# A mixture-of-experts kernel: experts' outputs added to their tokens' rows in DRAM by an indirect transfer in place of one-hot products on TensorE

## The chip, the core and the metric

The kernel runs on one core of a Trainium2 chip. The metric is the device time of one execution in microseconds; the kernel before takes 2354.62 us, the median of three runs (2351.31 to 2360.58). The engines of the core are TensorE (PE; its weight loads are PEld), VectorE (DVE), ScalarE (ACT), GpSimd (POOL) and SyncE (SP). Each has its own queue of instructions and works through it in order; sixteen DMA engines move data for all of them.

## What is computed

The reference is two blocks of a language model, one after the other, for one sequence of 512 tokens (528 with 16 meta tokens) of width 1024, all in float32. The change concerns the end of the first block, a feed-forward layer in which each of 16 experts chooses its 66 tokens:

```python
def one_group(hs):
    logits = jnp.einsum('ld,de->le', hs, w_router, preferred_element_type=jnp.float32)
    aff = jax.nn.softmax(logits, axis=-1)
    g, idx = lax.top_k(aff.T, cap)                       # 16 experts, cap = 66 tokens each
    xg = hs[idx]
    a = jnp.einsum('ecd,edf->ecf', xg, w_gate)           # [1024, 2048] per expert
    u = jnp.einsum('ecd,edf->ecf', xg, w_up)
    y = jnp.einsum('ecf,efd->ecd', jax.nn.silu(a) * u, w_down)
    y = y * g[..., None].astype(y.dtype)
    out = jnp.zeros((L, D), y.dtype).at[idx.reshape(-1)].add(y.reshape(-1, D))
    return out.astype(hs.dtype)
...
h = h + expert_choice_ffn(rms_norm(h, ffn_norm_g[l]), w_router[l], w_gate[l], w_up[l], w_down[l])
```

Before it stand an attention and a convolution, whose projection gives `h`; behind it two more layers (an mLSTM layer and a latent attention) that read `h` in full.

## The kernel before, in words

**Precision.** Every weight and activation is split into two float32r parts, high and low, that sum to the float32 value; a product of two such pairs is three matmuls (`TRIPLES`, line 26). ACT writes the high part `wh` of a weight (line 164), DVE the low part `wl` as a difference (line 165).

**The weight stream.** All weights are one long list of items of 1 MB. `w_dma` (lines 117 to 140) issues an item's transfer on SP's queue into a slot; `w_cv` splits it into two halves of 128x1024, each of which takes one of four buffers of `wh` and of `wl`; `w_get` hands an item to the products, keeps one item split ahead and, among the experts, up to `K.ring` = 17 items in transfer or waiting. A slot comes free once DVE has read it. The last 48 items (two experts) have ten slots, because seven (`ex1`) are given to the next layer.

**The router** (`route`, lines 562 to 807) finishes `h` for each of four tiles of 128 tokens (`K.xs`, kept in SBUF) and for the 16 meta tokens, writes the normalised rows to DRAM as `hn_d` on ACT's queue (line 656), chooses the tokens, and leaves their positions `K.idx`, shifted positions `K.fi` and weights `K.gate`, one column for each expert.

**The experts** (`experts`, lines 905 to 1058). The order of TensorE's instructions is pinned to that of the program (`K.pin`); those of the other engines are put in order by the framework's scheduler. For each expert `e` and each half `f` of the hidden width, 48 products give G and 48 give U (66 rows by 1024 columns in PSUM); ACT takes silu of G into the tile `sa` (line 993), DVE multiplies it by U (line 999), and TensorE transposes the result (`rows_66`) for the 96 products of Y. In the middle of Y the tokens of the next expert, gathered by GpSimd into `xg` (`gather`, line 897, an indirect transfer by the list `K.idx`), are transposed.

**The sums** (lines 939 to 960). After Y, ACT and DVE split the 66 rows of Y, times their weight, into `yh` (in the buffer `xg`) and `yl` (in the buffer `sa`, of which there is one), and DVE builds a one-hot matrix `oh` from `K.fi`. For each of four tiles of tokens, four products of `oh` with `yh` and `yl` put the rows where their tokens stand, and DVE adds them to `K.xs`. The generator `left` is advanced inside the next expert's first half: three of the four tiles behind G's items 1 to 3, the fourth behind U's first item. After the fourth, `gather(K, e + 2)` is issued. The last expert's sums come in front of the second block, with a share of its work (lines 1024 to 1048).

Of the kernel before, what the change touches and what calls it, by code (L numbers as in the profile page):

```python
# [8 lines left out]
F32 = mybir.dt.float32  # L9
# [3 lines left out]
AF = mybir.ActivationFunctionType  # L13
OP = mybir.AluOpType
# [39 lines left out]
class Kern:  # L54
# [17 lines left out]
    def load_vecs(self, pool):  # L72
        """vectors whose elements go to partitions: rows of one tile, transposed"""
        nc, A = self.nc, self.A
        srcs = {"cw": A["conv_w"][0] if "conv_w" in A else None, "sg": A.get("attn_subln_g"),
                "acw": A["a_conv_w_2"][0], "acb": A["a_conv_b_2"], "ahg": A["a_h_norm_2"],
                "kvn": A["kv_norm_2"][None, :], "bn": A["b_norm_2"],
                "fg": A["ffn_norm_g"] if "ffn_norm_g" in A else None,
                "kg": A["k_gain_2"][None, 0:128], "qg": A["b_q_gain_2"][:, 0:128]}
        rows = self.t(pool, [128, 128], F32, "vrows")  # L80
        nc.gpsimd.memset(rows, 0.0)
        self.vcol = {}
        r = 0
        for n, src in srcs.items():
            if src is None:
                continue
            k = src.shape[0] * src.shape[1] // 128
            nc.gpsimd.dma_start(rows[r:r + k], src.rearrange("a (c p) -> (a c) p", p=128))
            self.vcol[n] = (r, k)
            r += k  # L90
        self.vrows = rows

    def vecs(self, ps):
        """called once the identity is there"""
        pt = self.t(ps, [128, 512], F32, "T", 2)
        self.nc.tensor.transpose(pt[:, :128], self.vrows, self.ident)
        self.vec = self.t(self.cst, [128, 128], F32, "vec")
        self.nc.vector.tensor_copy(self.vec, pt[:, :128])
# [14 lines left out]
    # ---- weights: raw float32 in, split into two float32r parts that sum to it exactly  # L113
# [98 lines left out]
    def rsqrt(self, pool, v, name):  # L212
        """1 / sqrt(v), by Newton steps"""
        nc = self.nc
        p, k = v.shape
        y = self.t(pool, [128, k], F32, name, 2)[:p]
        t = self.t(pool, [128, k], F32, name + "t", 2)[:p]
        nc.vector.tensor_single_scalar(y.bitcast(I32), v.bitcast(I32), 1, op=OP.logical_shift_right)
        nc.vector.tensor_scalar(y.bitcast(I32), y.bitcast(I32), -1.0, float(0x5f3759df), op0=OP.mult, op1=OP.add)
        nc.vector.tensor_scalar_mul(v, v, -0.5)  # L220
        for _ in range(3):
            nc.vector.tensor_mul(t, y, y)
            nc.vector.tensor_mul(t, t, v)
            nc.vector.scalar_tensor_tensor(y, t, 1.5, y, op0=OP.add, op1=OP.mult)
        return y

    def rstd(self, pool, ms, n, name):
        """ms [p, k] sums of squares over n -> 1/sqrt(ms/n + eps)"""
        p, k = ms.shape
        v = self.t(pool, [128, k], F32, name + "v", 2)[:p]  # L230
        self.nc.vector.tensor_scalar(v, ms, 1.0 / n, EPS, op0=OP.mult, op1=OP.add)
        return self.rsqrt(pool, v, name)


    def rsqrt_s(self, pool, v, name):
        """1 / sqrt(v) from ScalarE's square root and one Newton step"""
        nc = self.nc
        p, k = v.shape
        y, t = (self.t(pool, [128, k], F32, name + x, 2)[:p] for x in "yt")
        nc.scalar.activation(t, v, AF.Sqrt)  # L240
        nc.vector.reciprocal(y, t)
        nc.vector.tensor_mul(t, y, y)
        nc.vector.scalar_tensor_tensor(t, t, -0.5, v, op0=OP.mult, op1=OP.mult)
        nc.vector.scalar_tensor_tensor(y, t, 1.5, y, op0=OP.add, op1=OP.mult)
        return y

    def rstd_a(self, pool, ms, n, name):
        """the same from exp(-ln / 2) and one Newton step, where ScalarE has the tables of both"""
# [12 lines left out]
class Halves:  # L261
    """two tiles [128, n, ..], indexed as one [128, 2 n, ..]"""
# [23 lines left out]
def interleave(*gens):  # L286
    """gens: (generator, total cost); advances the one that is least far along"""
# [14 lines left out]
def block1(K):  # L302
# [26 lines left out]
    # ---- norm and transpose, a tile of tokens at a time, each followed by its values  # L329
# [18 lines left out]
    def values(pair, w, t):  # L348
# [3 lines left out]
        if m < 128:  # L352
            # both parts of the few tokens at once
# [42 lines left out]
    def proj_T(w, j, put):  # L396
        """channels 128 j .. of the chunk: put(columns, [128, 264] in PSUM) for each half of the tokens"""
# [138 lines left out]
    # lambda  # L536
# [25 lines left out]
def route(K, mixed, pa):  # L562
    """mixer output, router, expert choice, keys and values of the memory; starts the experts' weights"""
# [13 lines left out]
    K.hn_d = nc.dram_tensor("hn_d", [L, D], F32, kind="Internal").ap()  # L577

# [15 lines left out]
    # position of a token in two parts, its affinity in three, all of them exact in bfloat16  # L594
# [8 lines left out]
    # both parts of the few tokens side by side  # L603
# [10 lines left out]
    def mix(w, n, tiles):  # L614
        """columns 256 n .. of the mixer's output, for some tiles of tokens, the last head last"""
# [22 lines left out]
    def router(t):  # L638
        """affinities from h times the gain; 1 / rms comes in with the softmax"""
# [16 lines left out]
        nc.scalar.dma_start(K.hn_d[c0:c0 + m], hn[:m])  # L656
        lo = K.t(ps, [128, 512], F32, "Rl")
# [63 lines left out]
    # the CAP largest of each row, equal ones in order of position  # L721
# [33 lines left out]
    # every expert's slots against every expert's columns, then each expert's own  # L755
# [54 lines left out]
def mem_load(K, gain, mt):  # L810
    """the memory and its gain"""
# [5 lines left out]
def mem_norm(K, p, gain, mt, ms, junk=None):  # L817
    """a tile of the memory, normalised"""
# [7 lines left out]
def mem_keys(K, p, l, mks):  # L826
    """the keys of the memory, normalised, times their gain and the queries'"""
# [31 lines left out]
def expert_items(K):  # L859
    """weights of the memory's keys and values, of the experts"""  # L860
# [19 lines left out]
    # some slots have another use at the end  # L880
# [16 lines left out]
def gather(K, e, xg=None):  # L897
    """the tokens of expert e"""
# [6 lines left out]
def experts(K):  # L905
# [9 lines left out]
    def rows_66(src, dst):  # L915
        """[CAP, 1024] transposed and split: [128, 8 CAP]"""
# [22 lines left out]
    def sums(y, e, tags, after):  # L939
        """expert e's part of the sum, by a product with its one-hot rows: a generator of four steps"""  # L940
# [12 lines left out]
        for t in range(4):  # L953
# [4 lines left out]
            if t == 3:  # L958
                gather(K, e + 2)
            yield  # L960

    def mem_T(t):
        """a tile of the memory, transposed and split"""
# [12 lines left out]
    for e in range(K.ne):  # L976
# [5 lines left out]
        for f in range(2):  # L982
            g = K.t(ps, [128, 2, 512], F32, "G")
            for j in range(4):
# [5 lines left out]
                if f == 0 and j > 0:  # L990
                    next(left, None)
# [3 lines left out]
            for j in range(4):  # L995
                gemm(u, xx, 2 * j, get(), j == 0, j == 3)
                if f == 0 and j == 0:
                    next(left, None)
# [20 lines left out]
        left = sums(y, e, "GU" if last and K.fuse else "T", ins)  # L1019
        next(left)  # L1020
# [3 lines left out]
    if K.fuse:  # L1024
        # the second layer's keys and values of the memory, while the sums come together
# [35 lines left out]
def rows_T(K, ps, dst, src, cols):  # L1061
    """token-major src [128, 1024] -> dst (two parts) [:, 0:8, cols]"""
# [8 lines left out]
def mem_q(K, p, ps, w, hT, dst):  # L1071
    """a chunk of mq -> normalised, times 128 ** -0.5, transposed and split, for two heads; dst(j): where to"""
# [32 lines left out]
def mem_fetch(K, p, l, h, bufs=1, raw=("m_raw", 1)):  # L1105
    """keys and values of the memory for head h of layer l"""
# [9 lines left out]
def mem_attn(K, p, ps, kv, qT, dst, tp="m_pT"):  # L1116
    """a head of the memory attention, times dst / 2, into dst [128, 512]"""
# [28 lines left out]
def silu2(K, p, dst, src):  # L1146
    """2 silu(src) = (tanh(src / 2) + 1) src"""
# [5 lines left out]
def softmax_T(K, p, ps, s, scale, nb):  # L1153
    """rows of softmax(scale * s), [128, 128 nb] in PSUM, transposed: [128 keys, nb, 128] in PSUM"""
# [18 lines left out]
def acc4(K, ps, n):  # L1173
    """accumulators for the four tiles of tokens"""
# [4 lines left out]
def mm_part(K, acc, hT, k0, w, nk, first, last):  # L1179
    """acc[t] += hT[:, k0 ..]^T w"""  # L1180
# [9 lines left out]
# the chunks that come last have the last turn  # L1190
# [3 lines left out]
def out_proj(K, ps, mixed, his, rest, final):  # L1194
    """mixed^T @ w, in parts of 256 columns: final(t, n, psum); rest(c), a tile for the rest of chunk c"""
# [51 lines left out]
def a_pre(K):  # L1247
    """what the first layer can have before its input is there"""
# [10 lines left out]
    # gate weights: i in columns 0..3, f in 32..35  # L1259
# [27 lines left out]
def a_squares(K, t):  # L1287
    """h times its gain, and the sums of the squares before and after"""
# [9 lines left out]
def block2_a(K):  # L1298
# [31 lines left out]
    # x = rms_norm(h, final_norm_g); rmsnorm(x, a_norm); the values of the first head  # L1330
# [11 lines left out]
    for t in range(4):  # L1342
# [4 lines left out]
        # 1 / rms(h) and 1 / (rms(h) rms(x)) from the two sums  # L1347
# [28 lines left out]
    # gates, rows of heads  # L1376
# [17 lines left out]
    # log weight of s in t: (i_s - b_s) + R_S[t], R_S[t] = b_t - m_t + the sums of the tiles S .. T - 1  # L1394
# [176 lines left out]
    def rest(c):  # L1571
        # in place of the chunk before
# [15 lines left out]
def block2_b(K, out):  # L1588
# [11 lines left out]
    # the last two heads of both kinds take the place of values  # L1600
# [65 lines left out]
    # gains: rows of the rope part, columns of the rest  # L1666
# [28 lines left out]
    # rope tables  # L1695
# [28 lines left out]
    def rope_rows(pool, dst, src, heads):  # L1724
        """[128, 4, heads, 64]"""
# [11 lines left out]
    # latents of keys and values, of queries; the rope part that the keys share  # L1737
# [48 lines left out]
    def gen_q(pr):  # L1786
        """queries of two heads"""
# [22 lines left out]
    def gen_kv(pr):  # L1810
        """keys and values of two heads"""
# [43 lines left out]
    def gen_attn(pr):  # L1855
        qT, kT, qpT, kpT, v, rq = qkv[pr]
        for hh in range(2):
            # keys c of queries t in part t + 3 c
# [46 lines left out]
    def rest(c):  # L1905
        # in place of the chunk before
# [12 lines left out]
    def part(t, cs, one=False):  # L1919
        nonlocal prev  # L1920
        for c in cs:
            for i, (a, b) in enumerate(TRIPLES):
                beg, end = c == 0 and i == 0, c == ORDER[-1] and i == 2
                # of two tiles in a bank the first one opens it, the second one closes it
# [12 lines left out]
    def gen_out():  # L1937
        """the first part of the columns, as far as the chunks are there"""
# [106 lines left out]
```

## Time and profile before

| what | value |
|---|---|
| median of three runs | 2354.62 us (2351.31 to 2360.58) |
| span of the profiled execution | 2354.2 us (the runs' median is 0.42 us above it) |
| TensorE busy | 2277.8 us, 97% |
| TensorE's weight loads busy | 1707.0 us, 73% |
| DVE busy | 1838.8 us, 78% |
| ACT busy | 1456.0 us, 62% |
| GpSimd busy | 212.3 us, 9% |
| DMA | 520.27 MB, mean 221 GB/s |
| TensorE's granted clock | 0.985 in the mean |

A line of the timeline gives start, duration, engine, line of the kernel, operation, output<-input by the program's names, shape, and in brackets how long the engine had stood idle and what released it. The windows view gives for each stretch the busy time (and the number of instructions) of PE, PEld, DVE, ACT and POOL, the granted clock, the DMA engines' share and the rate. Matmuls are pipelined: the duration of one is longer than its share of a sequence, so the cost of a product is read from a group's length divided by its count.

### The profile page before, as it was taken

The page shows a single profiled execution, that of the slowest core. Times are in us where ns is not written, and L with a number is a line of the kernel's source. Part 1 is how long each engine was busy: PE and PEld are TensorE (multiplying, and loading weights), DVE is VectorE, ACT ScalarE, POOL GpSimd, SP SyncE. Part 2 cuts the span into 40 slices and gives each one's busy share as a digit, 9 for nine tenths or more (in the row PEclk, how much of TensorE's full clock was granted, in tenths as well). Part 3 has the DMA queues.
Part 4 walks back from the last instruction along what each step waited for, and adds up shares of the span by engine and source line. Part 5 has one row for each costly group of instructions (what it writes and reads, how often), then busy time and mean ns, then how long its engine had stood idle before and what let it go on. Part 6 is the DMA issues. An engine that isn't in the chain of part 4 may idle for free.

```text
span 2354.2 us, 33846 instructions
## 1 busy us (share of the span) xinstructions
PE 2277.8 (97%) x12647; PEld 1707.0 (73%) x12647; DVE 1838.8 (78%) x2704; ACT 1456.0 (62%) x2182; POOL 212.3 (9%) x227
## 2 busy tenths in 40 slices
PE   7999888999999999999999999999999999899999
PEld 7899884666666666666666666688888899777779
DVE  5766576999999999999999999876666756676752
ACT  4554345777777777777787777755453634555551
POOL 2201261000000000000000110241000000010000
PEclk9999997999999999999999999999999999999999
DMA  5211767999999999999999799542322233211122
GB/s 179 80 54 55 254 217 287 362 361 354 349 355 357 358 360 355 349 353 356 361 358 357 284 333 351 197 144 86 117 72 72 81 125 114 69 51 60 50 90 72
DMA packets 201553, 520.27 MB, mean 221 GB/s; under 512 B 12527, under 2 KB 94061, under 8 KB 201389
## 3 DMA queue, kind: packets, MB, share of 16 engines
q1 hardware_dynamic: 196157, 507.64, 60.3%
q0 software_dynamic: 3232, 7.77, 1.1%
q10 hardware_dynamic: 2000, 2.71, 0.3%
q8 instruction: 99, 1.62, 0.3%
q14 instruction: 65, 0.53, 0.1%
HBM read 504.31 MB, written 11.60 MB: 219 GB/s over the span
## 4 chain that ended last, share of the span: by engine, by line
PE 80%; DVE 2%; ACT 1%; issue 0%; DMA 0%; SPq 0%; ACTq 0%; DVEq 0%
PE P L198 23%; PE G L198 15%; PE U L198 15%; PE Y L198 15%; PE S L198 4%; PE O L198 3%; PE T L198 3%; PE T L203 1%; PE T L1169 0%; PE T L1843 0%; DVE wl L165 0%; PE T L1136 0%; DVE x L1293 0%; PE T L1067 0%; DMA xg<-hn_d,idx 0%
## 5 line engine op out<-in xcount | busy, mean ns | idle before, releaser
L164 ACT ACTIVATE wh<-raw 128x1024 fp32r<-128x1024 f32 (+1 forms) x604 | 632.6, 1054 | 292.0 <-PE P L198 69.1
L165 DVE TENSOR_TENSOR wl<-raw,wh 128x1024 fp32r<-128x1024 f32 (+1 forms) x586 | 705.5, 1223 | 121.8 <-ACT wh L164 115.9
L198 PE MATMUL G<-wh,xgT 128*66 128x512 f32 x1024 | 281.0, 396 | 0.7 <-ACT xgT L191 0.7
L198 PE MATMUL Y<-wh,hT 128*66 128x512 f32 x1024 | 278.4, 394 | 0.0
L198 PE MATMUL U<-wh,xgT 128*66 128x512 f32 x1024 | 278.2, 393 | 0.0
L164 ACT ACTIVATE wh<-h 128x1024 fp32r<-128x1024 f32 x200 | 210.3, 1059 | 63.2 <-PE G L198 22.5
L198 PE MATMUL P<-hT,wh 128*128 128x512 f32 x768 | 247.8, 396 | 0.0
L165 DVE TENSOR_TENSOR wl<-h,wh 128x1024 fp32r<-128x1024 f32 x196 | 234.2, 1220 | 13.0 <-ACT wh L164 11.2
L198 PEld LDWEIGHTS U<-wh,xgT 128*66 128x66 f32 x1024 | 140.2, 137 | 95.3
L198 PEld LDWEIGHTS G<-wh,xgT 128*66 128x66 f32 x1024 | 140.0, 138 | 94.6 <-issue 1.6
L198 PEld LDWEIGHTS Y<-wh,hT 128*66 128x66 f32 x1024 | 137.6, 137 | 90.2
L198 PEld LDWEIGHTS P<-hT,wh 128*128 128x128 f32 x768 | 143.6, 188 | 29.2
L198 PE MATMUL Y<-wl,hT 128*66 128x512 f32 x512 | 159.9, 394 | 2.2 <-DVE wl L165 2.2
L198 PE MATMUL G<-wl,xgT 128*66 128x512 f32 x512 | 160.9, 396 | 0.6 <-DVE wl L165 0.6
L198 PE MATMUL U<-wl,xgT 128*66 128x512 f32 x512 | 160.0, 394 | 0.0
L198 PE MATMUL P<-wh,hT 128*128 128x256 f32 (+2 forms) x712 | 147.2, 289 | 5.4 <-ACT hT L191 3.2
L198 PE MATMUL P<-hT,wl 128*128 128x512 f32 x384 | 151.4, 394 | 0.0
L198 PE MATMUL P<-h,wh 128*128 128x264 f32 x640 | 126.1, 290 | 1.6 <-ACT qraw L415 1.0
L165 DVE TENSOR_TENSOR wl<-mx,wh 128x1024 fp32r<-128x1024 f32 x96 | 118.0, 1247 | 8.6 <-ACT wh L164 7.5
L198 PEld LDWEIGHTS P<-wh,hT 128*128 128x128 f32 x712 | 116.2, 190 | 7.4 <-ACT hT L191 3.9
L164 ACT ACTIVATE wh<-mx 128x1024 fp32r<-128x1024 f32 x96 | 100.8, 1059 | 30.0 <-PE U L198 9.3
L198 PE MATMUL P<-wl,hT 128*128 128x256 f32 (+2 forms) x408 | 116.1, 287 | 0.0
(646 smaller groups left out, 4116.4 us busy)
## 6 DMA issues: line engine op xcount, KB each, us to landing
raw<-w_gate SPq DMA_DIRECT2D x82, 1024.0 KB, 6.9
raw<-w_down SPq DMA_DIRECT2D x80, 1024.0 KB, 7.1
raw<-w_up SPq DMA_DIRECT2D x76, 1024.0 KB, 6.9
h<-w_up SPq DMA_DIRECT2D x35, 1024.0 KB, 6.8
h<-w_down SPq DMA_DIRECT2D x32, 1024.0 KB, 7.3
h<-w_gate SPq DMA_DIRECT2D x31, 1024.0 KB, 6.9
raw<-a_w_in SPq DMA_DIRECT2D x24, 1024.0 KB, 5.3
mx<-w_up SPq DMA_DIRECT2D x17, 1024.0 KB, 7.2
```

The lines of the kernel that those rows point to most:

```text
L164: self.nc.scalar.activation(hv, v[:, r], AF.Copy)
L165: lo.tensor_tensor(lv, v[:, r], hv.bitcast(F32), op=OP.subtract)
L198: self.last_mm = self.nc.tensor.matmul(out, l, r, start=st, stop=sp)
L203: i = self.nc.tensor.transpose(out, src, ident)
```

## The change

Experts 0 to 14 no longer use products for their sums. The router also writes `h` to a DRAM tensor `acc_d`. After Y of an expert, ACT writes the rows times their weights to `ys` (in the buffer `sa`), and GpSimd issues one indirect transfer that adds the 66 rows of `ys` to the rows `K.idx` of `acc_d`; the gather for expert e + 2 is issued behind it. After the scatter of expert 14, four transfers on GpSimd's queue load the tokens' rows of `acc_d` back into `K.xs`. Expert 15 keeps the products. The rest of the diff takes comments and docstrings away.

```diff
@@ route @@
     K.hn_d = nc.dram_tensor("hn_d", [L, D], F32, kind="Internal").ap()
+    K.acc_d = nc.dram_tensor("acc_d", [L, D], F32, kind="Internal").ap()
...
         nc.scalar.dma_start(K.hn_d[c0:c0 + m], hn[:m])
+        nc.scalar.dma_start(K.acc_d[c0:c0 + m], h[t])
@@ experts @@
             nc.vector.tensor_add(K.xs[t], K.xs[t], o.rearrange("p a b -> p (a b)"))
-            if t == 3:
-                gather(K, e + 2)
             yield
 
+    def scatter(y, e):
+
+        ys = K.t(p, [CAP, 2, 512], F32, "sa")
+        nc.scalar.activation(ys, y[:CAP], AF.Copy, scale=K.gate[:, e:e + 1])
+        nc.gpsimd.indirect_dma_start(out=K.acc_d, out_offset=bass.IndirectOffsetOnAxis(ap=K.idx[:, e:e + 1], axis=0),
+                                     in_=ys.rearrange("p a b -> p (a b)"), in_offset=None, compute_op=OP.add)
+        gather(K, e + 2)
+        if e == K.ne - 2:
+            for t in range(4):
+                nc.gpsimd.dma_start(K.xs[t], K.acc_d[NM + 128 * t:NM + 128 * t + 128])
...
                 if f == 1 and j == 0:
                     rows_66(hh, hT[0])
-                if f == 0 and j > 0:
-                    next(left, None)
...
                 gemm(u, xx, 2 * j, get(), j == 0, j == 3)
-                if f == 0 and j == 0:
-                    next(left, None)
...
-        left = sums(y, e, "GU" if last and K.fuse else "T", ins)
-        next(left)
+        if last:
+            left = sums(y, e, "GU" if K.fuse else "T", ins)
+            next(left)
+        else:
+            scatter(y, e)
```

## Rows read from the trace of the kernel before

**Rows 1.** Windows of the experts' stage (columns as told above).
```profile
400.00:450.00 50.00, 50.00 (x230) 30.23 (x229) 47.10 (x44) 39.35 (x41) 0.00 (x0) 1.00 1.00 379
450.00:1300.00 850.00, 850.00 (x3893) 520.62 (x3892) 800.77 (x711) 651.77 (x652) 20.55 (x12) 1.00 0.97 355
```

**Rows 2.** The chain of waits, pieces in order of time: start, us, what.
```profile
479.47 11.08 PE U L198 x48
...
1411.58 11.09 PE U L198 x48
```

**Rows 3.** Timeline, SP's issues and ACT's first reads of the same slots.
```profile
510.02 3.14 SPq L138 DMA_DIRECT2D mx<-w_down  x2
...
557.65 1.06 ACT L164 ACTIVATE wh<-mx 128x1024 fp32r<-128x1024 f32 x1 [0.32 <-PE U L198]
...
1406.46 3.25 SPq L138 DMA_DIRECT2D mx<-w_down  x2
...
1431.49 3.89 ACT L164 ACTIVATE wh<-mx 128x1024 fp32r<-128x1024 f32 x4
```

**Rows 4.** DMA issues: queue, operation, count, KB each, median us to landing.
```profile
raw<-w_gate SPq DMA_DIRECT2D x82, 1024.0 KB, 6.9
...
mv_d<-mv POOLq DMA_DIRECT2D x1, 512.0 KB, 8.2
```

**Rows 5.** The tile xg: the sums' products, and the gather's landing times (ns min/median/max).
```profile
L198 PE MATMUL T<-xg,hT x120: 391/395/403, 447.3 to 1463.2; 66*128 66x512 f32 x120
...
L198 PE MATMUL T<-sa,hT x120: 388/395/427, 447.5 to 1463.4; 66*128 66x512 f32 x120
...
DMA to landing us min/median/max: 4.4/8.2/9.6
```

**Rows 6.** Timeline of PE: the end of Y, the first and the last group of sums.
```profile
513.03 0.62 PE L198 MATMUL Y<-wl,hT 128*66 128x512 f32 x2
...
519.01 0.40 PE L198 MATMUL T<-xg,hT 66*128 66x512 f32 x1
...
519.97 1.11 PE L198 MATMUL G<-wh,xgT 128*66 128x512 f32 x4
...
530.22 0.39 PE L198 MATMUL T<-xg,hT 66*128 66x512 f32 x1
...
531.14 1.07 PE L198 MATMUL U<-wh,xgT 128*66 128x512 f32 x4
```

**Rows 7.** Windows view of one period of an expert.
```profile
479.47:551.18 71.71, 71.71 (x329) 43.91 (x328) 67.58 (x61) 54.98 (x56) 1.71 (x1) 1.00 0.96 358
```

**Rows 8.** DVE's groups in that period that belong to the sums (busy us, mean ns).
```profile
L957 DVE TENSOR_TENSOR x<-x,T 128x1024 f32<-128x1024 f32 x4 | 4.9, 1213 | 0.0
...
L950 DVE SCALAR_TENSOR_TENSOR sa<-Y,gate,xg 66x512 fp32r<-66x512 f32 x2 | 1.5, 742 | 0.0
...
L945 DVE TENSOR_TENSOR hT<-iota,fi 66x512 fp32r<-66x512 f32 x1 | 0.7, 681 | 0.0
```

**Rows 9.** Timeline of ACT after the end of Y.
```profile
514.20 0.67 ACT L949 ACTIVATE xg<-Y,gate 66x512 fp32r<-66x512 f32 x1
```

**Rows 10.** Timeline around a silu in a half without sums.
```profile
478.84 0.62 PE L198 MATMUL G<-wl,xgT 128*66 128x512 f32 x2
...
480.01 1.00 ACT L993 ACTIVATE sa<-G 66x1024 f32<-66x1024 f32 x1
...
480.91 2.00 ACT L164 ACTIVATE wh<-raw 128x1024 fp32r<-128x1024 f32 x2
...
481.99 3.51 DVE L165 TENSOR_TENSOR wl<-raw,wh 128x1024 fp32r<-128x1024 f32 x3 [0.62 <-ACT wh L164]
...
485.74 0.64 PE L198 MATMUL U<-wl,xgT 128*66 128x512 f32 x2
```

**Rows 11.** Timeline of ACT in the router: the last issue to hn_d.
```profile
326.58 0.33 ACTq L656 DMA_DIRECT2D hn_d<-hn  x1
327.50 1.06 ACT L164 ACTIVATE wh<-raw 128x1024 fp32r<-128x1024 f32 x1 [2.50 <-PE O L198]
```

## The prediction

> **What bounds the kernel now.** I began with the windows view, to find the stage that the change touches. From 400 to 1300 us, among the experts, the matmul unit is busy in all 50.00 of 50 and 850.00 of 850 us at a granted clock of 1.00, VectorE (DVE) in 94%, and the DMA engines show a share of 0.97 to 1.00 [rows 1]. Three resources are close to full: the next views must tell which sets the pace. The chain of waits does. It runs through TensorE alone, and the same step, U's 48 products, returns from 479.47 to 1411.58 us after thirteen experts [rows 2], so one expert takes (1411.58 - 479.47) / 13 = 71.70 us. 48 products take 11.08 us [rows 2], 0.2308 us each, so the 288 products of G, U and Y take 66.5 us, and the 16 products of the one-hot sums with three batches of transposes the other 5.2. That fills the period with no wait. The DMA is not the pace: SyncE issues a weight transfer at 510.02 us that ScalarE (ACT) first reads at 557.65 us [rows 3], 47.6 us later, while a transfer lands in 6.9 us [rows 4]. The queue waits for slots, and the weights lie ready for about 47.6 - 6.9 = 40 us.
>
> **What is removed.** The products T<-xg,hT and T<-sa,hT are 240 in all [rows 5], 16 for each of experts 0 to 14, in four groups within the next expert's G and U. From the first product of a group to the next weight product it is 519.97 - 519.01 = 0.96 us in the first group and 531.14 - 530.22 = 0.92 us in the last [rows 6]; four groups of 0.94 are 3.76 us. They lie on the path that sets the end, so 15 x 3.76 = **56.4 us** go, if TensorE stays fed; an expert then takes 67.9 us. DVE is busy for 67.6 us of a period [rows 7] and loses four additions, two splits and one comparison, 4.9 + 1.5 + 0.7 = 7.1 us [rows 8]: 60.5 of 67.9 remain, so it does not become the pace. ACT exchanges two half rows of 0.67 us [rows 9] for one of about 1.0 us (the silu of the same 66x1024 shape takes 1.00 [rows 10]); it is busy for 55.0 us [rows 7], and I cost that at nothing.
>
> **What is added in each expert: a transfer and a new wait.** The scaled rows `ys` take the single buffer `sa`. Its next writer is the next expert's first silu, which now waits until the scatter has landed; behind it in ACT's queue stand all weight conversions. GpSimd is free (1.71 us of work in a period [rows 7]), so its order, scatter and then the gather for e + 2, delays nobody; that gather is even issued earlier than today, behind Y instead of behind the fourth sum.
>
> When must the scatter be done? Call the end of Y T0; it is 513.03 + 0.62 = 513.65 us [rows 6]. G's 48 products then last 11.08 us. In a half without sums the silu starts 480.01 - 479.46 = 0.55 us after G's last product (478.84 + 0.62) [rows 10], so here at T0 + 11.6. How late may it be? After that silu two conversions start at 480.91 us, and DVE's split of the first, at 481.99, ends near 483.2 us (three take 3.51); TensorE wants that split at 485.74 [rows 10]. That is 2.5 us to spare: the deadline is **T0 + 14.1**. Past it TensorE waits one for one.
>
> When is it done? ACT first reads Y at 514.20 us [rows 9], T0 + 0.55, plus 1.0 us of work: GpSimd issues at T0 + 1.6, or at T0 + 3.6 if the scheduler puts two conversions (2.00 us [rows 10]) before it. No row shows an adding transfer. The nearest is the gather: the same 66 rows of 4 KB, the same list and queue, in the same crowd; it lands in 8.2 us at the median and in 9.6 at most [rows 5]. With 8.2 us the scatter lands at T0 + 9.8 to 11.8, with 9.6 at 13.2 at the latest: before the deadline, **0 us**, and I take that, by the nearest row. A gain is excluded, since a wait can give none. The upper bound takes twice the whole gather, 16.4 us, because an add has to read the old row too: T0 + 18.0 to 20.0, 3.9 to 5.9 us of stall, 15 times: 58 to 89 us.
>
> The Trainium skill says why an add is dearer than a copy (Collectives: The Full Stack, "The bandwidth ceiling: the fold count and why AG ≠ RS ≠ AR"): the adding transfer reads two sources for one write, so that a reduction ran at half the rate of a copy. No run here shows it yet; by it the part of the 8.2 us that is movement would double.
>
> **What is added once.** Five copies of h to `acc_d` on ACT's queue: an issue takes 0.33 us, together 1.7 us, beside an ACT that idles 2.50 us behind the last of today's issues [rows 11]. The bounds are 0 and 1.7; I take 0, for that idle time. They land long before the first scatter, one expert later. The four loads of 512 KB back into `xs` stand on GpSimd's queue behind the wait for scatter 14, near T0 + 12 of the last expert; such a transfer landed in 8.2 us [rows 4], and the first reader comes only after that expert's Y, more than 50 us later. The small GpSimd pieces of `a_pre2` that may queue behind them are not wanted before the last expert's second half. Cost 0; if all four went one after the other, 33 us, they would still be early. Their bytes are counted next.
>
> **The DMA's share.** Today 24 x 1.049 MB of weights and 0.27 MB of gather pass per expert. With the scatter's 0.27 MB twice (read and write) it is 25.98 MB in 67.9 us, 383 GB/s. The stretch at a full share of 1.00 moved 379; the long one moved 355 at 0.97 [rows 1], 366 at a full share. At 379 GB/s an expert needs 68.5 us: the weights fall behind by 0.6 us an expert, 9 us in all, and the reload of 2.1 MB costs 5.5 more. The 40 us of lead cover that. Near the end the ring has fewer slots: a transfer of 1406.46 us is first read at 1431.49 [rows 3], 25 us later, of which 18 are lead, still more than 14.5.
>
> **The sum.** The profiled execution's span is 2354.2 us, 0.4 below the runs' median of 2354.62: 2354.2 - 56.4 + 0 + 0 = 2297.8, and 0.4 above that in a run's time: **2298 us**.
>
> **Rivals.** (1) **The DMA becomes the pace.** For it: the share of 0.97. Against it: 379 GB/s in a stretch in which TensorE waited for nothing [rows 1]. With 366 GB/s an expert needs 71.0 us, 15 x 3.1 + 5.7 - 40 = 12 us are lost: 2310. With 355 as the ceiling it needs 73.2: 15 x 5.3 + 5.9 - 40 = 45 us lost, 2343, hardly a change. I give it 0.10. The Trainium skill has a rule for this (SBUF — State Buffer, "Summary: rules for kernel authors"): reckon some 358 GB/s between HBM and SBUF. By it the estimate would be 72.6 us an expert and 2334 us; the 379 GB/s above disagree with it.
>
> (2) **The scatter lands after the deadline but takes less than was removed**: between T0 + 14.1 and T0 + 17.9. The middle, 15 x 1.9 = 28 us of stall, gives 2326 us. For it: the transfer meets a full DMA; against it: the gather's worst is 9.6 us. 0.10.
>
> (3) **Slower.** The silu of every expert waits for its scatter past T0 + 17.9, the point from which the stall exceeds the 3.76 us removed. At the upper bound it stalls 3.9 to 5.9 us: 15 x 0.14 to 15 x 2.14, so 2357 to 2387 us, the middle 2372. For it: the chain read, add, write, whose price no row shows, and a buffer that has no second copy. Against it: it needs twice the gather's whole time. 0.14.
>
> **How the numbers follow.** My forecast has 0.60; its own range is 2292 to 2305, as the runs shown lie up to 6 us from their median and 1.7 us of issues stand open. The other 0.06 is a change that all but vanishes because the scheduler orders the other engines anew. A measurement of this kernel can tell about 0.5%, 12 us, from no change. Faster by more: 0.60 + 0.10 + most of (1) = 0.78; within it 0.08; slower 0.14. For 8 in 10 the range leaves out rival (3) and reaches over (1) and (2): 2292 to 2345.
>
> **What would show it.** Right: U's 48 products return every 67.9 us; no T<-sa,hT among TensorE's groups in experts 0 to 14; the scatter lands within 12 us of its issue and ACT's wait for it at the silu stays under 3 us. Wrong: TensorE idle in front of U's products with ACT's wh as releaser and the scatter as ACT's, a period above 69 us, a landing more than 12.5 us after issue (the deadline less T0 + 1.6); or wh waiting for the weights' transfers, which would be rival (1).

## The result and the profile after

The changed kernel takes 2325.3 us (median of 4 runs, 2316.9 to 2327.4) beside 2353.1 us of the kernel before in the same runs: a ratio of 0.986, 95% interval 0.983 to 0.989. It is faster by 28 us. 56 were forecast: half of the gain is missing, and this section and the next ask where it went. The profiled execution took 2327.35 us, with a span of 2325.6 us.

The windows view of the changed kernel, the stretches of [rows 1] (PE, PEld, DVE, ACT and POOL busy, granted clock, DMA share, GB/s):

```profile
400.00:450.00 50.00, 50.00 (x236) 30.21 (x235) 45.96 (x41) 40.20 (x41) 3.44 (x2) 1.00 1.00 373
450.00:1300.00 850.00, 832.47 (x3810) 497.67 (x3809) 759.09 (x648) 669.28 (x659) 41.24 (x24) 1.00 1.00 370
```

TensorE, without a gap before, now stands idle for 850 - 832.47 = 17.5 us of the long stretch, at an undiminished clock. DVE fell from 94% to 89%, ACT rose from 77% to 79%. The DMA share rose to 1.00, which makes the DMA a suspect.

The chain of waits of the changed kernel, the same step as in [rows 2] (start, us, what):

```profile
478.33 11.08 PE U L198 x48
...
1315.31 11.08 PE U L198 x48
1383.21 11.08 PE U L198 x48
```

The period is not uniform. The first twelve take (1315.31 - 478.33) / 12 = 69.75 us each, but the last one, up to expert 14, takes 67.90, the forecast's number. So experts 2 to 13, and 15 as will be seen, carry 1.85 us that the forecast does not have. The products T<-xg,hT and T<-sa,hT of [rows 5] are gone. One of those periods in the chain:

```profile
512.52 11.07 PE G L198 x48
523.59 9.24 PE U L198 x40
...
532.85 1.07 ACT wh L164
...
533.94 1.24 DVE wl L165
...
535.20 1.01 ACT sa L1002
...
536.26 2.97 PE G L198 x12
```

G's 48 products end at 523.59, and the silu of that G, which takes `sa`, runs only at 535.20 us, after U is all but done. The second half's G, which needs the same PSUM buffer, waits for it. The timelines of PE and of ACT (start, us, what, idle time before and releaser), and who waited for that silu in the whole execution (us, times):

```profile
534.04 0.62 PE L198 MATMUL U<-wl,xgT 128*66 128x512 f32 x2
...
536.26 1.14 PE L198 MATMUL G<-wh,xgT 128*66 128x512 f32 x4 [1.59 <-ACT sa L1002]
```

```profile
513.06 1.10 ACT L965 ACTIVATE sa<-Y,gate 66x1024 f32<-66x1024 f32 x1
...
534.24 1.06 ACT L164 ACTIVATE wh<-raw 128x1024 fp32r<-128x1024 f32 x1 [0.33 <-PE U L198]
535.20 1.00 ACT L1002 ACTIVATE sa<-G 66x1024 f32<-66x1024 f32 x1
```

```profile
  PEld G L198: 27.0, 13
  PE G L198: 20.7, 13
```

Thirteen waits, of 1.6 us on PE; most of the rest of the 1.85 us lies in the products behind the stall, of which 12 take 2.97 us where 36 take 8.32. The silu has no idle time in front of it, so it waits for no landing: ACT simply reaches it late, behind 16 conversions. In the kernel before, the silu of a half without sums stood right behind G [rows 10]. The first half's own silu, the one in question, did not: it waited for the sums' last product, which also read `sa`, and ran 17.1 us after the scaling of Y began (514.20 us [rows 9]), behind 10 conversions. Nobody waited for it. ACT's timeline of the kernel before:

```profile
531.34 1.02 ACT L993 ACTIVATE sa<-G 66x1024 f32<-66x1024 f32 x1 [0.33 <-PE T L198]
```

In the changed kernel it runs 22.1 us after the scaling copy (513.06 to 535.20). Was the scatter late all the same? POOL's timeline, and the landing times of the transfers that read `sa` (min/median/max us):

```profile
504.50 1.97 POOL L903 DMA_INDIRECT xg<-hn_d,idx  x1 [56.42 <-PE T L203]
514.46 1.51 POOL L966 DMA_INDIRECT acc_d<-sa,idx  x1 [7.99 <-DMA xg<-hn_d,idx]
```

```profile
DMA to landing us min/median/max: 8.1/8.2/9.3
```

Issued at 514.46, it landed near 514.46 + 8.2 = 522.7 us, a microsecond before G was done and 12.5 us before the silu ran.

The loss adds up. The spans differ by 28.6 us: 56.4 removed; 13 x 1.85 = 24.0 given back in the stalls; 2.6 us fewer gained up to expert 1's U, which starts 1.14 us earlier where one expert's 3.76 were due (the first 200 us ran at a granted clock of 0.98 where before they had 1.00, ahead of all that was changed); 3.2 more behind the seam to block 2; 2.0 less in the last expert with that seam (1.5) and by rounding (0.5).

### The profile page after: what moved, and what is told of

The parts are those of the page before. It is cut to its first block, busy times and chain, and to the rows that moved or that the text cites. A ratio compares the mean times of both kernels' runs of the same rounds, so it can differ in the third digit from the quotient of the medians.

```text
span 2325.6 us, 33331 instructions
## 1 busy us (share of the span) xinstructions
PE 2228.5 (96%) x12407; PEld 1663.0 (72%) x12407; DVE 1764.5 (76%) x2599; ACT 1456.4 (63%) x2167; POOL 233.5 (10%) x246
## 4 chain that ended last, share of the span: by engine, by line
PE 78%; ACT 3%; DVE 2%; DMA 1%; issue 1%; POOL 0%; SPq 0%; ACTq 0%; DVEq 0%; POOLq 0%
PE P L198 23%; PE G L198 16%; PE Y L198 15%; PE U L198 14%; PE S L198 4%; PE O L198 3%; PE T L203 1%; DVE wl L165 1%; ACT wh L164 1%; ACT sa L1002 1%; PE T L1179 0%; DMA pos<-positions 0%; PE T L1853 0%; PE T L1146 0%; PE T L1077 0%
## 5 line engine op out<-in xcount | busy, mean ns | idle before, releaser
L165 DVE TENSOR_TENSOR wl<-h,wh 128x1024 fp32r<-128x1024 f32 x196 | 239.4, 1236 | 26.6 <-ACT wh L164 23.0
```

The lines of the kernel that those rows point to most:

```text
L165: lo.tensor_tensor(lv, v[:, r], hv.bitcast(F32), op=OP.subtract)
```

## The experiments

**Theory A**: the place of the first half's silu in ACT's order is the loss. The scheduler puts it behind U's conversions because `sa` hangs on a transfer; the transfer itself is early enough. **Theory B**: the landing holds the silu back. **Theory C**: the DMA is at its limit, and the period would not come down to 67.9 without the stalls either. Edits are against the changed kernel; line numbers move with them.

The table has three stretches of each trace, for what follows: start of U's second-half products in expert 1, their period from there to expert 14, and from there to the first long group of block 2's products (106 in a row), which covers the last expert and the seam. "Place" is how many conversions ACT's queue has between the scaling copy and the first half's silu.

| kernel | place | expert 1 at | period | seam | span | median of runs |
|---|---|---|---|---|---|---|
| before | 10 | 479.47 | 71.70 | 156.6 | 2354.2 | 2353 to 2359 |
| changed | 16 | 478.33 | 69.61 | 153.2 | 2325.6 | 2325.3 |
| e1 | 8 | 476.96 | 67.91 | 159.1 | 2304.2 | 2306.4 |
| e2 | 6 | 475.83 | 68.00 | 153.3 | 2293.2 | 2298.4 |
| e5 | 16 | 477.40 | 69.60 | 155.1 | 2321.5 | 2326.0 |
| e9 | 14 | 475.52 | 67.91 | 155.9 | 2299.2 | 2305.4 |
| e6 | 6 | 475.29 | 67.96 | 158.4 | 2302.7 | 2307.2 |

(In the changed kernel and in e5 and e9, experts 1 and 14 have places of 11 or 8. In the kernel before and in e1, e2, e6 and e9 an expert or two, mostly the last, differs by one to three.)

### e1: the scaled rows in another buffer

```
-        ys = K.t(p, [CAP, 2, 512], F32, "sa")
+        ys = K.t(K.pools["ex"], [CAP, D], F32, "xg").rearrange("p (a b) -> p a b", a=2)
```

> Scaled outputs in one of the buffers xg instead of the single buffer sa; the first half's silu then depends on no transfer, and the scheduler places it 8 conversions behind the scaling copy instead of 16. Theory A (the silu's place in ACT's order is the loss: 13 stalls of 1.83 us, the period with the stall 69.73, without it 67.9): period 67.9 to 68.0 for every expert, no 1.14 us in front of G's second-half products, 2325 - 24 = 2301, range 2297 to 2305. Theory B (the landing of the adding transfer holds the silu back): the same 2301, since this edit takes that wait away too; e2 and e5 tell A from B. Theory C (DMA sets the pace once the stall is gone: 25.98 MB a period at the 376 to 381 GB/s of the windows after the change make 68.2 to 69.1 us): period 68.2 to 69.1, the lead of the weight transfers shrinking from expert to expert, 2305 to 2317.

Measured: 2306.4 us, ratio 0.979 (0.977 to 0.982). By the time alone that lies in theory C's range and just above the 2305 of A and B; the period has to decide. The chain of waits of e1:

```profile
476.96 11.08 PE U L198 x48
...
1359.74 11.08 PE U L198 x48
```

(1359.74 - 476.96) / 13 = 67.91 us: the period is the forecast's, and theory C falls (the missing microseconds are in the table's seam, 159.1 us). The weights' lead shows why. Timelines of SP and ACT in e1, a slot's issue and its first reading as in [rows 3], early and late among the experts:

```profile
507.52 3.14 SPq L138 DMA_DIRECT2D mx<-w_down  x2
...
551.34 1.06 ACT L164 ACTIVATE wh<-mx 128x1024 fp32r<-128x1024 f32 x1 [0.32 <-PE U L198]
...
1353.24 3.25 SPq L138 DMA_DIRECT2D mx<-w_down  x2
...
1377.80 1.06 ACT L164 ACTIVATE wh<-mx 128x1024 fp32r<-128x1024 f32 x1 [0.31 <-PE Y L198]
```

43.8 us early and 24.6 late, beside 47.6 and 25.0 before. Theory C asked for a lead that shrinks from expert to expert, and it does not: a transfer issued at 1180.59 us is first read at 1225.38, 44.8 us later; the 24.6 belong to the end, where the ring has fewer slots. A full DMA, and yet the weights lie ready nearly as long as before. Between A and B this run cannot decide, since it removes the wait as well.

### e2: the same buffer, the silu put early

```
             u = K.t(ps, [128, 2, 512], F32, "U")
+            early = K.hold is None and f == 0 and 0 < e
+            if early:
+                K.hold = silu
             for j in range(4):
                 gemm(u, xx, 2 * j, get(), j == 0, j == 3)
+                if early and j == 0:
+                    K.hold = None
```

> The buffer sa is kept, so the first half's silu still waits for the adding transfer; only the conversions of U's first item are issued behind the silu on ACT, which puts it 6 conversions behind the scaling copy instead of 16. Theory A (place, not landing): the transfer, issued 1.4 us after the scaling copy starts and landing 8.2 us later, is there about 9.7 us after the copy's start; G's products end about 10.5 us after it; so ACT waits less than 1 us for the transfer, period 67.9 to 68.2, 2301, range 2297 to 2306. Theory B (the landing is what comes late): ACT stands idle in front of the silu for several us with the adding transfer as the releaser, the conversions queued behind it come late, TensorE stalls in front of U, period 69.5 or more, 2322 or more.

Measured: 2298.4 us, ratio 0.976 (0.973 to 0.979), the fastest of all and clear of the changed kernel's interval. ACT's timeline in e2, and what its silus waited for (us, times):

```profile
510.56 1.09 ACT L965 ACTIVATE sa<-Y,gate 66x1024 f32<-66x1024 f32 x1
...
521.12 1.02 ACT L1002 ACTIVATE sa<-G 66x1024 f32<-66x1024 f32 x1 [2.18 <-PE G L198]
```

```profile
  PE G L198: 30.5, 14
  DMA acc_d<-sa,idx: 2.8, 1
```

The silu now stands behind G, waiting for G in 14 experts and for the scatter in one, 0.6 us longer than the usual 2.18. With the wait in place and the silu early, the loss is gone: theory B falls.

### e5: no wait, the silu put late

e1's buffer, and for experts 2 to 13 and 15:

```
-            silu = nc.scalar.activation(hh, g[:CAP], AF.Silu)
             u = K.t(ps, [128, 2, 512], F32, "U")
             ...
+            K.w_cv()
+            with tc.issue_after(K.last_cv.ins):
+                silu = nc.scalar.activation(hh, g[:CAP], AF.Silu)
```

> The buffer of e1 (the silu depends on no transfer), but the first half's silu is issued behind U's conversions, 16 behind the scaling copy, for experts 2 to 13 and 15, where it stands in the changed kernel. Theory A (place): period 69.7 again, 1 to 1.3 us idle in front of the second half's products of G with ACT's silu as the releaser, 2325, range 2320 to 2329. Theory B (landing): nothing waits for the landing here, so the period is 67.9 and the time 2301, as e1.

Measured: 2326.0 us, ratio 0.987 (0.984 to 0.990): the changed kernel's time, though no silu depends on any transfer. ACT's timeline in e5, and who waited for its late silus:

```profile
533.31 1.06 ACT L164 ACTIVATE wh<-raw 128x1024 fp32r<-128x1024 f32 x1 [0.33 <-PE U L198]
534.27 1.00 ACT L1011 ACTIVATE sa<-G 66x1024 f32<-66x1024 f32 x1
```

```profile
  PEld G L198: 27.0, 13
  PE G L198: 20.7, 13
```

The same thirteen waits to the tenth of a microsecond. The place alone makes the loss.

### e9: two conversions earlier

e5 without the line `K.w_cv()`: the silu stands behind the conversions that U needs, ahead of the two that belong to the next G.

> e5 with the first half's silu two conversions earlier: 14 behind the scaling copy in experts 2 to 13 (right behind the conversions that U itself needs, ahead of the two for the second half's G); expert 15 keeps 16. Theory A, in numbers: in e5 U's products end at 534.7 in the period that was looked at, the two conversions take 2 x 1.39 us, so the silu ends at about 533.5 instead of 535.3, before U's products do, and the buffer G is free in time: no stall in experts 2 to 13, period 67.9 to 68.1, one stall left in expert 15, 2303 to 2310. Rival (any place behind U's conversions costs TensorE the silu's own 1 us): period 68.9, 2316 to 2320.

Measured: 2305.4 us, ratio 0.979 (0.976 to 0.981). ACT's timeline in e9:

```profile
528.65 1.06 ACT L164 ACTIVATE wh<-raw 128x1024 fp32r<-128x1024 f32 x1 [0.34 <-PE U L198]
529.62 1.00 ACT L1010 ACTIVATE sa<-G 66x1024 f32<-66x1024 f32 x1
530.52 1.99 ACT L164 ACTIVATE wh<-raw 128x1024 fp32r<-128x1024 f32 x2
```

The period is 67.91 us, and nobody waited for a silu, not in expert 15 either, where a stall was expected to stay (its silu has 17 conversions ahead of it, but several follow each other without a gap, and it runs 19.9 us behind the copy, not 22.1 as in e5). Two places in a queue separate no loss from all of it. The silu ends at 530.6, before U's products do at 531.7, so the buffer is free in time. ACT makes up the silu's microsecond from the 0.3 us that it idles before each conversion.

### e3, e4, e7: what the adding transfer costs where nothing waits

e3 is e1 without the transfer, e4 has a plain write in its place, e7 issues it twice.

> e1 with the adding transfers left out: the outputs of experts 0 to 14 are computed and scaled but never added to the tokens' rows, so the result lacks them. Theory A (the transfers are hidden): within 3 us of e1, period 67.9. Theory C (they cost DMA time that is short: 66 rows of 4 KB read and written, 0.54 MB of 26 MB a period, 2%): up to 1.4 us a period less than e1, about 20 us less over 15 experts, if e1's period is above 67.9; otherwise the same.

Measured: 2305.9 us, ratio 0.979 (0.976 to 0.982), as e1. Leaving the transfers out gains nothing. The periods are 67.91 us to 747 us; from there the scheduler's order differs from e1's, and they are 68.6 us, with the conversions behind the silu late by some 0.4 us in each half. So the comparison of the whole times is good to some 6 us only; that of the early periods is exact.

> e1 with every adding transfer issued twice, so the outputs of experts 0 to 14 are added twice; no engine waits for either. If the adding transfers are hidden with room to spare, the period stays 67.9 and the time within 5 us of e1's 2306. If DMA is at its limit at this pace (share 1.01 and 378 to 382 GB/s in e1's windows), a further 0.27 MB written, and as much read if the adding reads it, take 0.7 to 1.4 us a period, 11 to 21 us in all, 2317 to 2327, with TensorE waiting for conversions and those for weights.

Measured: 2304.6 us, ratio 0.976 (0.973 to 0.980), and a period of 67.91 us. Two stretches of the windows view of e7:

```profile
400.00:600.00 200.00, 200.00 (x922) 120.42 (x921) 182.03 (x158) 161.14 (x160) 14.13 (x8) 1.00 1.02 380
...
1000.00:1200.00 200.00, 200.00 (x922) 120.42 (x921) 181.49 (x157) 161.15 (x160) 14.03 (x9) 1.00 1.02 384
```

TensorE is busy in every microsecond with twice the adding traffic. The DMA share of 1.00 was no limit: more was moved at the same pace. By e1's leads the queue is full because it runs ahead into free slots.

> e1 with a plain indirect write in place of the adding one, so the result holds only the last expert's outputs per row. The transfers' packets fall from 0.33 us towards the 0.16 us that undisturbed copies show, if it is the adding that makes them long; landing and time within 0.5% of e1 either way, since nothing waits for them.

Measured: one run, 2310.2 us, a period of 67.91 us. The queue that carries all indirect transfers (packets, MB, share of 16 engines) and the issues of the scatters alone (count, median us to landing); first e1, then e4:

```profile
q0 software_dynamic: 5488, 13.93, 2.4%
...
acc_d<-xg,idx POOLq DMA_INDIRECT x15, 9.2
```

```profile
q0 software_dynamic: 5488, 13.93, 1.9%
...
acc_d<-xg,idx POOLq DMA_INDIRECT x15, 7.2
```

The time came as expected, the landing did not: with the adding it is 2.0 us longer at the median (7.8 to 10.0 us beside 6.8 to 8.0). By the share, the 15 x 66 packets of the rows are longer by about 0.5% x 16 x 2304 / 990 = 0.19 us each (0.15 to 0.22 with the rounding of the share). In a window around one transfer the queue takes 13.1% of 16 engines for 10.51 us in e1 and 8.7% for 7.82 us in e4; put on the 66 rows, that is 0.33 and 0.16 us a row.

### e8: a landing that really is late

e2 with the adding transfer issued twice from `sa`.

> e2 with every adding transfer issued twice from the single buffer sa, so the outputs of experts 0 to 14 are added twice and the first half's silu waits for the later of two landings. The silu of e2 runs 10.6 us behind the scaling copy's start and has 2.5 us to spare by the prediction, so the deadline is about 13.1 us behind it. If the two transfers run side by side, the second lands about 1.5 us later than the single one (9.7), at 11.2 to 12: ACT waits about 1 us, TensorE does not, and the time is e7's change on top of e2, within 5 us if that is nothing. If they run one after the other (two landings of 8.2 us in a row, about 18 to 19.5), the deadline is passed by 5 to 6.4 us, TensorE stands idle in front of U for that in each of 15 periods, 75 to 96 us more, 2373 to 2395.

Measured: 2440.4 us, ratio 1.034 (1.031 to 1.038). GpSimd issues the second transfer only when the first has landed. Timelines of POOL and ACT in e8:

```profile
522.23 1.46 POOL L967 DMA_INDIRECT acc_d<-sa,idx  x1 [7.99 <-ACT sa L965]
530.89 1.46 POOL L967 DMA_INDIRECT acc_d<-sa,idx  x1 [7.20 <-DMA acc_d<-sa,idx]
```

```profile
520.82 1.10 ACT L965 ACTIVATE sa<-Y,gate 66x1024 f32<-66x1024 f32 x1
...
539.01 1.02 ACT L1003 ACTIVATE sa<-G 66x1024 f32<-66x1024 f32 x1 [9.80 <-DMA acc_d<-sa,idx]
...
597.15 1.10 ACT L965 ACTIVATE sa<-Y,gate 66x1024 f32<-66x1024 f32 x1
```

This is how a late landing looks: idle time in front of the silu, with the transfer named. The silu runs 18.2 us behind the copy, as expected of two landings, 7.6 later than in e2; yet this period (520.82 to 597.15) is 76.3 us, 8.4 more than 67.9, and the mean over all (copies from 442.5 to 1524.5 us, 14 periods of 77.3) is 9.4 more (with a silu 7.9 us late in the mean), where 5 to 6.4 were expected. Two things were missed. PE's timeline and the windows of e8 show them:

```profile
541.03 1.97 PE L198 MATMUL U<-wh,xgT 128*66 128x512 f32 x4 [6.92 <-ACT wh L164]
```

```profile
531.20:534.10 2.90, 2.90 (x13) 1.50 (x11) 0.00 (x0) 0.00 (x0) 1.15 (x1) 1.00 1.03 421
534.10:541.00 6.90, 0.01 (x1) 0.00 (x0) 0.00 (x0) 1.99 (x3) 0.00 (x0) 0.71 0.64 217
541.00:545.00 4.00, 3.97 (x12) 2.31 (x13) 3.99 (x4) 3.91 (x5) 0.00 (x0) 0.64 0.15 24
```

TensorE stood for 6.92 us, so behind this silu only 7.6 - 6.92 = 0.7 us were to spare and not 2.5 (e2's order has two conversions fewer ahead of it). And the granted clock fell during the idle time and was 0.64 over the next 4 us, a mean of 0.50 (1.2 GHz) up to 543 us and 1.00 (2.4 GHz) from 544 us, so the first products took 1.97 us for four instead of 1.08. Over the 14 periods TensorE waits for 100.4 us in all in front of U, 7.2 a period; by that, 2.2 of the 9.4 are left for products at the lower clock.

### e6: both edits

> The two edits of e1 and e2 together: scaled outputs in a buffer xg, and the conversions of U's first item issued behind the first half's silu. If the early place alone is what counts, the period is 67.9 and the time that of e2, 2298, range 2293 to 2304; if the silu's wait for the adding transfer in the buffer sa cost something in e2 (one wait of 2.8 us in its trace), 1 to 3 us less than e2; if it was the last expert and not the place that made e2 faster than e1, then the time moves with the order the scheduler finds there, up to 2306.

Measured: 2307.2 us, ratio 0.979 (0.976 to 0.981). The period is 67.96 us. That of e2 is 68.00, because the one expert whose silu waited for the scatter took 68.45 (copies at 918.36 and 986.81 us): the wait cost at most some 0.5 us, once. The time is e1's, because the seam and the stretch from there to the end are: 158.4 and 785.5 us in e6, 159.1 and 785.4 in e1, beside 153.3 and 780.1 in e2. The chain of waits of e1 in the last expert:

```profile
1409.72 5.01 PE U L198 x20
1414.79 0.42 DVE wl L165
...
1437.19 3.43 DVE wl L165
1440.66 3.46 PE U L198 x14
```

For 26 us it runs through conversions and block 2's small vector work that the scheduler puts among them. The place of the silu does not set e2 ahead of e1, since e6 has e2's place and e1's time. That the order found for the seam does is likely, and for the stretch behind it nothing is shown.

## Why the prediction was half right

- **The bound and the removal: right.** Without the late silu the period is 67.91 us (e1, e9, e7), 3.79 less than before; 3.76 were forecast. Nothing else became the pace.
- **The landing: right.** Forecast T0 + 9.8 to 11.8; it was T0 + 10.2 in the period shown (T0 = 511.89 + 0.62 = 512.51, landed at 522.7), 8.2 us at the median and 9.3 at most. The upper bound, twice the gather, was not reached: beside a plain write the add cost 2.0 us of landing (e1, e4). The Trainium skill's half rate for a reduction (Collectives: The Full Stack, "The bandwidth ceiling: the fold count and why AG ≠ RS ≠ AR"), stated there for collectives, agrees with what a row took on the DMA engines, 0.33 us against 0.16; the landing did not double.
- **The step that failed: "so here at T0 + 11.6".** The silu's start was carried over from a half without sums of the kernel before, as if its place in ACT's queue were given. The first half's own silu already stood elsewhere there, at 531.34, T0 + 17.7, behind another wait for `sa`. In the changed kernel it ran at 535.20, T0 + 22.7. The prediction asked when the new wait would *end*, and not where the scheduler would *put* an instruction that has such a wait. Behind 16 conversions instead of e1's 8, the silu freed the PSUM buffer G 1.6 us late, 13 times. e5 shows that the place suffices for the loss, e2 and e9 that without it there is none.
- **The deadline was the wrong one.** "2.5 us to spare" was counted for U's products, whose conversions stand behind an early silu. A late silu has them ahead of it and cannot delay U; then the next need is the second half's G, whose buffer the silu must free. In e9 the silu runs 8 us later than in e1 and costs nothing, in the changed kernel 11 us later and costs 1.85. The prediction had no price for that.
- **Rival (2) has the right time, 2326 us, by the wrong cause.** No silu of the changed kernel waited for a landing. That the measured time lies within 2292 to 2345 is luck in this sense: the range reached up over rivals that did not occur. Nearest to the cause was the remainder of 0.06, "the scheduler orders the other engines anew", which had neither a mechanism nor a price.
- **Rival (1), the DMA: rightly small.** e7 moved 380 to 384 GB/s with no wait of TensorE; the rule of some 358 GB/s (the Trainium skill, SBUF — State Buffer, "Summary: rules for kernel authors") is exceeded here.
- **Rival (3)** had the mechanism that e8 forces, but "one for one" is too cheap: a silu late by 7.9 us in the mean left TensorE idle for 7.2 and cost 9.4 us a period, as the granted clock fell.
- **POOL's order was the other way round**: the gather went ahead of the scatter. It cost nothing. The copies of h and the reload of `xs` cost nothing that the variation from run to run (expert 1's U at 475 to 481 us in the table's kernels and in e7) lets one see.

What stays open: why the scheduler puts that silu behind exactly 16 conversions. It does so when `sa` is handed to a transfer, and doesn't when it isn't (e1); its reckoning was not looked into.

## What to carry to other kernels

When a change hands a buffer to a transfer, ask of the buffer's next user not only when its wait ends but where its engine will run it, and read that order in the trace: an instruction with no idle time in front of it that still releases a stall is late by its place, and is cured by the order, not by a faster transfer. Look past the first reader to whatever else the instruction frees; here a PSUM buffer one half further on. A DMA share of 1.00 with a lead that does not shrink is a queue that runs ahead, not a bound.

## What the runs showed of the hardware

An indirect transfer of 66 rows of 4 KB that adds, beside one that writes (e1 and e4): 9.2 us of landing instead of 7.2, 0.33 us instead of 0.16 of a DMA engine's time for a row, and 1.50 us instead of 0.95 of POOL's time. The bytes moved count the add once (0.27 MB each, e7 against e1). TensorE's granted clock stayed at 1.00 through idle times of 1.6 us in the changed kernel, and fell to 0.50 during one of 6.9 us in e8, which made a stall dearer than its length.
